# Convolution by pairs of tokens, VectorE in written order through the attention, and other places and times for output weights and norms, in one layer of a streaming encoder

## The chip, the cores and the metric

The kernel runs on one core of a Trainium2 chip. The metric is the device time of one execution in microseconds (us); lower is better. Before the change the median of three executions is 1045.45 us (1045.14 to 1045.65).

The engines are called as the profile calls them: PE multiplies matrices, DVE (VectorE), ACT (ScalarE) and POOL (GpSimd) work on whole tiles of 128 rows, SP only issues transfers (DMAs). Each has a queue of its own and works through it in order; semaphores tie the queues together. A DMA can add to its destination while it writes; this kernel issues those from POOL's queue.

## The reference, cut to what matters

One layer: an RMS norm, one input projection, and from its columns two branches.

```python
glu, q, k, v = project(rmsnorm(xp, norm_mix[l]), w_in[l])      # glu = a * sigmoid(b), 512 channels
glu_ext = concat([zeros((bsz, 30, 512)), glu], axis=1)         # or the last 30 rows of a running stream
a_out = silu(layernorm(depthwise_causal_conv(glu_ext, dw_w, dw_b)))   # 31 taps, each channel by itself
attn = prompt_attention(q, k, v, ...)                          # 16 chunks of 64 tokens, 8 heads, 16 meta tokens
xp = xp + concat([a_out, attn]) @ w_out[l]
```

Then follow a gated feed-forward (2816 wide, with a short convolution of its own) and a last norm. A second, small stream of 32 tokens with cached keys and values goes through the same layer. All values are float32. The kernel keeps tokens on the free axis: 16 meta tokens, 1024 prompt tokens and 32 of the running stream, 1072 columns, with channels on the 128 rows.

## The kernel before, in words

**Precision.** PE multiplies in a rounded form of float32, so each operand is split into a high and a low part, and each product is three matmuls: high by high, low by high, high by low (`mm3`, L257 to L262). A high part is a copy on ACT. A low part (value minus high part) is either one subtraction on DVE, or a negated copy on ACT followed by a transfer on POOL's queue that adds the value (`wload`, `wsplit`, L224 to L251).

**Input projection, 0 to about 160 us.** Columns of tokens are cut into three blocks `TB`. Weight tiles `c` = 0 to 13 are worked in a fixed order (`ORDER`): gate and value of convolution channels 0 and 1 first, then keys, values, channel 2, queries; the two weight tiles 6 and 7 of channel 3 are left for later. DVE takes the results out of PSUM (`in_evac`), and as soon as a channel `p` (128 rows of channels) has its gated value in a block, its convolution is put on a queue (`taps_of`, `conv_taps`): 31 taps, each one DVE instruction over the columns of a segment (`SEGS`), multiply by a weight and add (L405 the first, L408 the others). `taps(us)` issues taps worth about so many microseconds from up to two segments in turn. Twenty taps of one segment of channel 0 are done by ACT and adding transfers instead (`chain_taps`), and `chain_end` (L437) adds their two sums on DVE.

**Attention, about 164 to 248 us.** A loop of 20 rounds (L1012 on) carries 18 jobs: the meta tokens, 16 chunks, the running stream. In round `i` job `i` gets its scores on PE (L807), its bias and row minimum on DVE (`soft_a`, L762) and its exponentials on ACT (L769); job `i-1` gets its normalisation (`soft_b`, L774 and L777, or L779 where ACT does it: `SCA[i]` of four tiles), its transposes on PE (L826, L828) and their copies on ACT (L833); job `i-2` gets its output on PE (L842, L846) and the copy into `CA` on ACT (`keep`, L850). Between them PE does `FILL[i]` steps of the two left weight tiles (`glu_stream`; a step is three matmuls), first all blocks of tile 6, then all of tile 7. When these are done, `after_glu` splits `CA` and the second output weight tile, and PE starts on the output projection of the attention branch for block 0 (`ah_stream`, `AH[i]` steps in the last seven rounds). `taps(TA[i])` issues convolution taps at each round's end.

PE and ACT run in the order in which the program writes their instructions (`MANUAL`). DVE's order is chosen at build time by a list scheduler, in which taps have low priority and fill gaps.

**Output projection, about 248 to 345 us.** Twenty groups (L1123 on) multiply the attention half by output weight tiles `m2` = 0 to 3 for token blocks 1, 2 and 0. Each group is four steps, and each step is a tick. Ticks drive the layer norms of the convolution branch (`ln`, one for each block: sums, mean, squares, root, scaling, silu, split), which may begin at tick 14, with 21 ticks between beginnings and once their taps are issued. ACT copies each group's result out of PSUM (`ah_add`, L988), an adding transfer adds the layer's input. Then `conv_half` multiplies the normed convolution by the convolution half of the output weights (`whl`), in the order `WOC`, adds on DVE (L1170) and prepares the feed-forward. Three of these weight tiles are split only after the twenty groups (L1146), and the split tiles of the normed convolution (`CVH`, `CVL`) get their place when all three norms have summed their squares, by giving up the tile `glu` (`open_cv`).

Weight tiles pass through two raw buffers (`fetch`) and two pairs of high and low buffers; a third pair of uses waits for the first.

**Feed-forward, 345 us to the end.** Dense matmuls; the change does not touch it.

Of the kernel before, what the change touches and what calls it, by code (L numbers as in the profile page):

```python
# [18 lines left out]
P = 128  # L19
# [70 lines left out]
AFE = (0, 3, 18, 19)  # L90
GXW = FW - 1 + NPR + FW - 1 + NS
GOW = GXW - (FW - 1)
GS = NPR + FW - 1
# [81 lines left out]
def body(nc, tc, cp, wp, xp, dp, io):  # L175
# [10 lines left out]
    def close(cm):  # L186
        cm.__exit__(None, None, None)
# [209 lines left out]

    tapq, spare = [], [0.0, 0]

    def conv_taps(p, a0, a1, b):  # L400
        e, a = glu[:, p, :], acc[:, p, a0:a1]

        def tap(k):
            if k == 0:
                nc.vector.tensor_scalar(out=a, in0=e[:, a0:a1], scalar1=pcol("cw", p * CW), scalar2=pcol("cb", p),  # L405
                                        op0=ALU.mult, op1=ALU.add)
            else:
                nc.vector.scalar_tensor_tensor(out=a, in0=e[:, a0 + k:a1 + k], scalar=pcol("cw", p * CW + k),  # L408
                                               in1=a, op0=ALU.mult, op1=ALU.add)
# [26 lines left out]

    def chain_end():  # L437
        for a, half in chain:
            nc.vector.tensor_tensor(out=a, in0=a, in1=half, op=ALU.add)
        chain.clear()  # L440

    def taps(us, behind=None):
# [125 lines left out]
    def lead(c, b):  # L568
        return H0 if c >= 10 and b == 0 else 0
# [138 lines left out]
    def take(dst=None, dve=False):  # L708
        return wsplit(raws.pop(0), dst, dve)
# [205 lines left out]
            Chunk.keep(self, n=NS)  # L915

    def glu_stream():
        w = nxt
        for i, c in enumerate(order[NPRE:]):
            for b in range(3):  # L920
                for k, ps in enumerate(in_mm(b, w, lead(c, b))):
                    if k == 2 and b == 0:
                        wn = take()
                    if k == 2 and b == 1:
                        fetch()
                    if k == KD - 1:
                        pend.append((c, b, ps))
                    yield
            w = wn
        woas.append(w)  # L930
# [5 lines left out]
    def ca_split(b, k0, k1, dma=False):  # L936
        t0, n = OB[b]
        for k in range(k0, k1):
            if dma:
                nc.scalar.copy(CAH[b][:, k, :], CA[:, k, t0:t0 + n])  # L940
                nc.scalar.activation(CAL[b][:, k, :], CA[:, k, t0:t0 + n], AF.Copy, scale=-1.0)
            else:
                split(CAH[b][:, k, :], CAL[b][:, k, :], CA[:, k, t0:t0 + n])
        if dma:
            nc.gpsimd.dma_start(CAL[b][:, k0:k1, :], CA[:, k0:k1, t0:t0 + n], accum_op=ALU.add)

    def after_glu():
        nonlocal X, cX, cS
        close(cH)
        cX, px = pool("x1", "right")  # L950
        X = [new(px, f"x{b}", KD, n) for b, (t0, n) in enumerate(OB)]
        cS, pcs = pool("cas", "right")
        for b, (t0, n) in enumerate(OB):
            CAH.append(new(pcs, f"cah{b}", 4, n, dt=F32R))
            CAL.append(new(pcs, f"cal{b}", 4, n, dt=F32R))
        for step in AG:
            for op in step:
                if op == "h":
                    raw = raws.pop(0)
                    hi, lo = (wp.tile([P, 1024], F32R, tag=t, name=t) for t in ("whi", "wlo"))  # L960
                    nc.scalar.copy(hi, raw)
                elif op == "l":
                    nc.scalar.activation(lo, raw, AF.Copy, scale=-1.0)
                    nc.gpsimd.dma_start(lo, raw, accum_op=ALU.add)
                    woas.append((hi, lo))
                    fetch()
                else:
                    while op[0] == "1" and kept[0] < 11:
                        yield
                    ca_split(int(op[0]), int(op[1]), int(op[1]) + 2, op in CSD)  # L970
                    halved[0] += op[0] == "0"
            yield

    def halves(w):
# [34 lines left out]
    left = (len(order) - NPRE) * 3 * KD - PF  # L1009
    for _ in range(PF):  # L1010
        next(stream)
    for i in range(len(jobs) + 2):  # L1012
        job = jobs[i] if i < len(jobs) else None
        if a:
            a.soft_b(SCA[i])
        if job:
            job.scores()
            job.soft_a()
            job.exps(0)
            job.exps(1)  # L1020
# [12 lines left out]
        taps(TA[i], (job or a or z).q[1][3])  # L1033
        if not left and not pend and not defer:
            for _ in stream:
                pass
            next(later, None)
            ticks = len(jobs) + 2 - i
            for _ in range(AH[-ticks] if ticks <= len(AH) else 0):
                next(ahs, None)  # L1040
            for q in adds:
                ah_add(*q)
            adds.clear()
        if i == CHE:
            with tc.issue_after(job.q[1][3]):
                chain_end()
        z, a = a, job
    for _ in later:
        pass
    for _ in ahs:  # L1050
        pass
    for q in adds:
# [2 lines left out]
    def ln(b):  # L1055
# [31 lines left out]
        while not CVH:  # L1087
            yield 1
        for p in range(NCV):
            with tc.high_priority(offset=-1000000) if b else nullcontext():  # L1090
# [1 line left out]
                    split(CVH[b][:, p, lo_:hi_], CVL[b][:, p, lo_:hi_], acc[:, p, o:o + hi_ - lo_])  # L1092

    ca_split(2, 0, 4)
    close(cD)
    close(cA)
    lns = [ln(b) for b in range(3)]
    ticks, begun, due = [0], [], []

    def tick():  # L1100
        ticks[0] += 1
        for b, g in enumerate(lns):
            if len(due) == b:
                if ticks[0] < LN0 or begun and ticks[0] < begun[-1] + LNS or any(t[0] <= b for t in tapq):
                    return
                begun.append(ticks[0])
# [4 lines left out]
    whl, wres, squared, CVH, CVL = {}, [], [], [], []  # L1111

    def open_cv():
        nonlocal cG
        close(cG)
        cG, pd = pool("d3", "left")
        for b, (t0, n) in enumerate(OB):
            CVH.append(new(pd, f"cvh{b}", 4, n, dt=F32R))
            CVL.append(new(pd, f"cvl{b}", 4, n, dt=F32R))
        for m in range(2):  # L1120
            wres.append((new(pd, f"wrh{m}", 1024, dt=F32R), new(pd, f"wrl{m}", 1024, dt=F32R)))

    groups = [(m2, i, b) for m2 in range(2) for b in (1, 2) for i in range(2)]  # L1123
    groups += [(2, i, b) for i in range(2) for b in range(3)] + [(3, i, b) for b in range(3) for i in range(2)]
    for g, (m2, i, b) in enumerate(groups):
        if m2 not in woav:
# [12 lines left out]
        if len(squared) == 3 and not CVH:  # L1139
            open_cv()  # L1140
    if not CVH:
        taps(1e9)
        while len(squared) < 3:
            tick()
        open_cv()
    for m2 in WOC[1:]:  # L1146
        whl[m2] = halves(take((None, None, *wres)[m2], WLD))
        fetch()

    close(cS)  # L1150
    cH, ph = pool("h3", "right")
# [43 lines left out]
    region.__exit__(None, None, None)  # L1195
    close(cG)
    close(cC)
    cT, pt_ = pool("t", "left")
# [846 lines left out]
```

## Time and profile before

| | before |
|---|---|
| median of three executions | 1045.45 us |
| the profiled execution's own time | 1044.83 us |
| its span, first to last instruction | 1043.1 us |
| busy: PE, DVE, ACT, POOL | 1025.4, 880.8, 535.1, 189.5 us |
| convolution taps on DVE (L408), in 190 instructions | 155.3 us |
| granted TensorE clock | 0.998 |

The profiled execution is 0.62 us below the median, and 1.73 us of it lie outside the span. In the tables of stretches, each row is a stretch in us from the span's start, its length, the busy time of each engine with the number of instructions, the granted clock as a share, the busy share of the DMA engines and GB/s. In lists of groups, a row gives line, engine, operation, output and input, shape and count, then busy time and mean ns of one, then idle time ahead of them and what ended it. In lists of waits, a row gives who waited for whom, the total, the number of times, and the longest. In listings by time, a row begins with start and duration, and the time in square brackets is idle time ahead of it; durations of neighbours overlap a little, so the step from one to the next is somewhat shorter than the duration. Only PE's idle time lengthens the run for certain, since PE is busy for 98% of the span; idle time elsewhere counts where PE ends up waiting for it.

### The profile page before, as it was taken

Reading aid. Unit: us, or ns where it says so; the run is one execution under the profiler, and the core shown is the slowest. Engines: PE = TensorE matmul, PEld = TensorE weight load, DVE = VectorE, ACT = ScalarE, POOL = GpSimd, SP = SyncE. Lnnn points to the kernel's source line nnn. Section 1 sums busy time; section 2 is a strip of 40 time slices with the busy share of each in tenths; the row PEclk is TensorE's granted clock in tenths of the full one; section 3 lists DMA queues with packets and bytes.
Section 4 is the critical chain, followed back from the end, with each engine's and each line's share of the span. In section 5 each row is a group of like instructions: output and inputs, shape, how many; then the busy total and the mean of one; then the engine's idle time right before and its main releaser. Section 6 shows DMA issues by size and latency. Waiting matters only on the chain.

```text
span 1043.1 us, 20158 instructions
## 1 busy us (share of the span) xinstructions
PE 1025.4 (98%) x7699; PEld 999.2 (96%) x7699; DVE 880.8 (84%) x1723; ACT 535.1 (51%) x1146; POOL 189.5 (18%) x243
## 2 busy tenths in 40 slices
PE   9999999989999999999999999999999999999997
PEld 8999998758999999999999999999999999999997
DVE  7999988899978988989988989889888966986636
ACT  8653335897676744443543544445436722532334
POOL 1123120002425321020211111111100041000043
PEclk9999999999999999999999999999999999999999
DMA  7378673123963226244445445435536785732204
GB/s 269 90 167 162 148 151 89 41 52 62 168 165 106 81 83 158 73 130 144 117 129 156 121 123 155 132 114 146 152 93 231 247 171 138 252 122 81 83 1 167
DMA packets 77528, 137.39 MB, mean 132 GB/s; under 512 B 11248, under 2 KB 46184, under 8 KB 77432
## 3 DMA queue, kind: packets, MB, share of 16 engines
q1 hardware_dynamic: 58632, 100.96, 29.1%
q0 software_dynamic: 18368, 34.74, 19.7%
q8 instruction: 60, 0.98, 0.4%
q10 hardware_dynamic: 432, 0.41, 0.1%
q14 instruction: 36, 0.29, 0.1%
HBM read 81.52 MB, written 27.51 MB: 105 GB/s over the span
## 4 chain that ended last, share of the span: by engine, by line
PE 86%; ACT 6%; DVE 5%; DMA 2%; issue 1%; DVEq 0%; ACTq 0%
PE mm L1335 49%; PE mm L260 10%; PE mm L261 10%; PE mm L262 10%; PE mm L1546 3%; ACT pb L769 1%; DVE acc L408 1%; ACT glu L833 1%; PE R L297 1%; ACT hi L346 1%; PE R L1546 1%; PE R L276 1%; DMA raw<-woc 1%; DMA xs<-xT 0%; ACT glu L769 0%
## 5 line engine op out<-in xcount | busy, mean ns | idle before, releaser
L408 DVE SCALAR_TENSOR_TENSOR acc<-glu,prm,acc 128x324 f32<-128x324 f32 (+4 forms) x190 | 155.3, 847 | 1.1
L1335 PE MATMUL mm<-bh,sl 128*128 128x264 f32 (+1 forms) x664 | 148.4, 285 | 0.3 <-DVE x L1482 0.3
L1335 PE MATMUL mm<-bh,wlo 128*128 128x264 f32 (+1 forms) x560 | 134.5, 284 | 0.0
L1335 PE MATMUL mm<-th,rawr 128*128 128x264 f32 x640 | 122.5, 284 | 0.0
L1335 PE MATMUL mm<-bl,sl 128*128 128x264 f32 (+1 forms) x424 | 120.6, 284 | 0.0
L1335 PEld LDWEIGHTS mm<-bh,sl 128*128 128x128 f32 x664 | 112.1, 188 | 0.6 <-DVE x L1482 0.5
L260 PE MATMUL mm<-hi,whi 128*128 128x352 f32 (+3 forms) x312 | 104.0, 333 | 0.6 <-ACT hi L346 0.6
L1482 DVE TENSOR_TENSOR x<-x,mm 128x264 f32<-128x264 f32 (+7 forms) x222 | 69.4, 343 | 41.3 <-PE mm L1335 41.1
L261 PE MATMUL mm<-lo,whi 128*128 128x352 f32 (+3 forms) x312 | 101.3, 325 | 0.2 <-DVE lo L347 0.2
L1335 PEld LDWEIGHTS mm<-th,rawr 128*128 128x128 f32 x640 | 101.4, 188 | 0.0
L262 PE MATMUL mm<-hi,wlo 128*128 128x352 f32 (+3 forms) x312 | 101.2, 324 | 0.0
L1335 PEld LDWEIGHTS mm<-bh,wlo 128*128 128x128 f32 x560 | 97.8, 188 | 0.0
L1335 PE MATMUL mm<-tl,rawr 128*128 128x264 f32 x320 | 90.9, 284 | 0.0
L1223 ACT CAST sl<-x 128x512 fp32r<-128x512 f32 (+2 forms) x66 | 40.0, 608 | 95.1 <-PE mm L1335 79.7
L1335 PE MATMUL mm<-th,sl 128*128 128x264 f32 x344 | 85.9, 284 | 0.0
L1335 PEld LDWEIGHTS mm<-bl,sl 128*128 128x128 f32 x424 | 79.8, 188 | 0.0
L1335 PE MATMUL mm<-th,wlo 128*128 128x264 f32 x272 | 77.3, 284 | 0.0
L1335 PE MATMUL mm<-tl,sl 128*128 128x264 f32 x272 | 77.2, 284 | 0.0
L1335 PE MATMUL mm<-bh,whi 128*128 128x264 f32 (+1 forms) x312 | 71.8, 284 | 0.0
L1335 PEld LDWEIGHTS mm<-th,sl 128*128 128x128 f32 x344 | 61.0, 188 | 0.2 <-ACT gx L1480 0.2
L260 PEld LDWEIGHTS mm<-hi,whi 128*128 128x128 f32 x312 | 58.7, 188 | 1.8 <-ACT hi L346 0.8
L1335 PEld LDWEIGHTS mm<-tl,rawr 128*128 128x128 f32 x320 | 60.3, 188 | 0.0
(442 smaller groups left out, 3070.4 us busy)
## 6 DMA issues: line engine op xcount, KB each, us to landing
x<-wup SPq DMA_DIRECT2D x48, 256.0 KB, 2.8
yq<-x SPq DMA_DIRECT2D x46, 264.0 KB, 3.0
x<-wup SPq DMA_DIRECT2D x20, 512.0 KB, 3.4
wlo<-raw POOLq DMA_DIRECT2D x16, 512.0 KB, 4.6
ca<-ca POOLq DMA_DIRECT2D x18, 383.0 KB, 5.2
raw<-win SPq DMA_DIRECT2D x12, 512.0 KB, 4.7
raw<-wdn SPq DMA_DIRECT2D x12, 512.0 KB, 6.6
rb<-yq SPq DMA_DIRECT2D x10, 528.0 KB, 4.7
```

The costliest lines, as they stand in the source:

```text
L260: nc.tensor.matmul(ps, whi(k), xhi(k), start=first and i == 0, stop=False)
L261: nc.tensor.matmul(ps, whi(k), xlo(k), start=False, stop=False)
L262: nc.tensor.matmul(ps, wlo(k), xhi(k), start=False, stop=last and i == n - 1)
L276: nc.tensor.matmul(ss[:, i:i + 1], z[:, at:at + P], ones[:, 0:1], start=j == 0, stop=j == len(parts) - 1)
L297: nc.tensor.matmul(R[:, at:at + P], left[i], diag[i], start=True, stop=True)
L346: hid[b, k] = nc.scalar.activation(HI[b][:, k, :], X[b][:, k, :], AF.Copy, scale=pcol("g1", k)).ins
L408: nc.vector.scalar_tensor_tensor(out=a, in0=e[:, a0 + k:a1 + k], scalar=pcol("cw", p * CW + k), in1=a, op0=ALU.mult, op1=ALU.add)
L769: nc.scalar.activation(qs_[i], qs_[i], AF.Exp, bias=m[0][:, i:i + 1], scale=-1.0, accum_out=m[1][:, i:i + 1])
L1223: nc.scalar.copy(hi, raw)
L1335: nc.tensor.matmul(ps, w[:, j, :], x[:, j, :], start=first and j + i == 0, stop=j == 3 and i == 2, skip_group_check=True)
L1482: summed[0] = nc.vector.tensor_tensor(out=z, in0=z, in1=ps[:, lo_:hi_], op=ALU.add).ins
L1546: nc.tensor.matmul(ps, z[:, j, :], x[:, j, :], start=q in FIRST and j + i == 0, stop=j == 1 and i == 2, skip_group_check=True)
```

## The change

- **Pairs.** For channels 1 and 2 and the longer part of channel 3, the 31 taps over all columns become 48 instructions over half as many columns, reading and writing every second column. With a weight array of differences, even and odd outputs share the products of odd weights with sums of neighbouring inputs.
- **Written order.** In the attention loop DVE runs in the program's order too. Low parts, results out of PSUM and taps move ahead of the outputs and transposes in each round; results out of PSUM are taken one round later. `TA` is smaller.
- **Attention's side work.** Six rounds leave all normalisation to DVE. Low parts of `CA` and of three weight tiles go to DVE; their negated copies and adding transfers go. `glu_stream` takes block by block both tiles instead of tile by tile. `chain_end` becomes two adding transfers, two rounds earlier.
- **Output weights and norms.** The third output weight tile gets buffers of its own. The first eight groups go block by block. The convolution's weights are split after groups 13, 15 and 17 and at the end, two of them with adding transfers. Norms begin at ticks 15, 39, 59. Block 0 of the normed convolution has its place from the start; the others come over `glu`.

```diff
-TA = [2.01, 2.74, 5.63, 6.64, 4.22, 3.28, 2.42, 2.68, 2.08, 1.57, 2.08, 2.08, 3.18, 1.41, 2.1, 0.85, 4.71, 3.21, 5.98, 2.57]
+TA = [0.0, 0.0, 2.0, 1.0, 1.9, 1.5, 2.0, 1.5, 1.2, 1.2, 0.4, 1.0, 0.5, 1.0, 0.5, 0.9, 0.9, 1.2, 3.0, 3.0]
-WOC = (0, 2, 1, 3)
-WLD = True
+WOC = (0, 2, 3, 1)
+WLD = (False, False, True, True)
-SCA = [1, 2, 2, 2, 1, 1, 2, 2, 2, 2, 2, 1, 2, 2, 0, 1, 1, 2, 2, 2]
-LN0 = 14
-LNS = 21
+SCA = [1, 2, 2, 2, 1, 1, 2, 2, 2, 2, 2, 1, 0, 0, 0, 0, 0, 0, 2, 2]
+LNT = (15, 39, 59)
-CHE = 5
+CHE = 3
-SEGS = (((0,), (1, 2)), ((0, 1, 2),), ((0, 1, 2),), ((0,), (1,), (2,)))
-CSD = ['12', '00']
+SEGS = (((0,), (1, 2)), ((0, 1, 2),), ((0, 1, 2),), ((0,), (1, 2)))
+PAIRS = ((1, 0), (2, 0), (3, 1))
+NP2 = CW // 2
-AG = (('00', '02'), ('h',), ('l',), ('10',), ('12',))
-AT = (1, 8)
-AT2 = 13
-AFE = (0, 3, 18, 19)
+AG = (('00',), ('02',), ('h',), ('l', '10'), ('12',))
+AT = {1: True, 8: False}
+AT2 = {13: 0, 15: 2, 17: 3}
+AFE = (0, 2, 9, 14, 16)
...
+    def pair_taps(p, a0, a1, b):
+        n = (a1 - a0) // 2
+        sums = pair_place(p, n + NP2 - 1)
+        y = [acc[:, p, a0 + i:a1:2] for i in range(2)]
+
+        def e(k, m=n):
+            return glu[:, p, a0 + k:a0 + k + 2 * m - 1:2]
+
+        def one(out, x, w, into):
+            nc.vector.scalar_tensor_tensor(out=out, in0=x, scalar=w, in1=into, op0=ALU.mult, op1=ALU.add)
+
+        def tap(k):
+            i, j = k
+            if i == 0:
...
+                nc.vector.tensor_tensor(out=sums, in0=e(1, m), in1=e(2, m), op=ALU.add)
+            elif i == 1:
+                w, x = pcol("cw", p * CW + 2 * j + 1), sums[:, j:j + n]
+                if j == 0:
+                    nc.vector.tensor_scalar(out=y[1], in0=x, scalar1=w, scalar2=pcol("cb", p), op0=ALU.mult,
+                                            op1=ALU.add)
+                else:
+                    one(y[1], x, w, y[1])
+            elif i == 2:
+                w = pcol("cw", p * CW) if j == 0 else pdif[:, p - 1, 0, j - 1:j]
+                one(y[0], e(2 * j), w, y[0] if j else y[1])
+            else:
+                w = pdif[:, p - 1, 1, j:j + 1] if j < NP2 else pcol("cw", p * CW + CW - 1)
+                one(y[1], e(2 * j + 1), w, y[1])
+
+        ks = [(0, 0), *((1, j) for j in range(NP2)), *((i, j) for j in range(NP2 + 1) for i in (2, 3))]
+        tapq.append([b, n, tap, ks, p])
...
     def chain_end():
         for a, half in chain:
-            nc.vector.tensor_tensor(out=a, in0=a, in1=half, op=ALU.add)
+            nc.gpsimd.dma_start(a, half, accum_op=ALU.add)
...
+    def low(lo, x, hi):
+        lows.append(lambda: nc.vector.tensor_tensor(out=lo, in0=x, in1=hi.bitcast(F32), op=ALU.subtract))
...
+            hi, lo, x = CAH[b][:, k, :], CAL[b][:, k, :], CA[:, k, t0:t0 + n]
+            nc.scalar.copy(hi, x)
+            low(lo, x, hi)
...
+    region.__exit__(None, None, None)
+    region = tc.manual_schedule(engines=MANEND)
+    region.__enter__()
     for i in range(len(jobs) + 2):
...
+        low_parts()
+        flush()
+        taps(TA[i])
         if z:
             z.outs()
         if a:
...
-        flush()
-        taps(TA[i], (job or a or z).q[1][3])
-        if not left and not pend and not defer:
+        if not left:
             for _ in stream:
                 pass
+            flush()
+            flush()
             next(later, None)
...
-    groups = [(m2, i, b) for m2 in range(2) for b in (1, 2) for i in range(2)]
+    groups = [(m2, i, b) for b in (1, 2) for m2 in range(2) for i in range(2)]
...
         if g in AT:
-            woas.append(take())
-        if g == AT2:
-            whl[0] = halves(take(dve=WLD))
+            woas.append(take(wthird if AT[g] else None))
+        if g in AT2:
+            conv_weights(AT2[g])
```

More of the change, by code (lines that the diff above doesn't have):

```diff
@@ L398, in body, with pair_place @@
     tapq, spare = [], [0.0, 0]
+    pdif = cp.tile([P, NCV - 1, 2, NP2], F32, tag="pdif", name="pdif")
+    co = PRM["cw"][0] + CW
+    wv = prm[:, co:co + (NCV - 1) * CW].rearrange("p (a b) -> p a b", b=CW)
+    nc.gpsimd.tensor_tensor(out=pdif[:, :, 0], in0=wv[:, :, 2::2], in1=wv[:, :, 1::2], op=ALU.subtract)
+    nc.gpsimd.tensor_tensor(out=pdif[:, :, 1], in0=wv[:, :, 0:CW - 1:2], in1=wv[:, :, 1::2], op=ALU.subtract)
+    def pair_place(p, n):
+        return (None, acc[:, 3, ACCW - n:], acc[:, 3, 0:n], glu[:, 2, 0:n])[p]
+    def pair_taps(p, a0, a1, b):
[9 more added lines that the diff above has]
+            if i == 0:
+                assert not any(q[4] == p - 1 and (p == 3 or len(q[3]) > 2 * (NP2 + 1)) for q in tapq if q[2] is not tap)
+                m = n + NP2 - 1
+                nc.vector.tensor_tensor(out=sums, in0=e(1, m), in1=e(2, m), op=ALU.add)
[14 more added lines that the diff above has]
+        tapq.append([b, n, tap, ks, p])
     def conv_taps(p, a0, a1, b):
+        if (p, b) in PAIRS:
+            pair_taps(p, a0, a1, b)
+            return
         e, a = glu[:, p, :], acc[:, p, a0:a1]
@@ L917, in glu_stream @@
     def glu_stream():
[L918 to L925, printed above, removed]
+        cs = order[NPRE:]
+        ws = {cs[0]: nxt}
+        for b in range(3):
+            for c in cs:
+                for k, ps in enumerate(in_mm(b, ws[c], lead(c, b))):
+                    if k == 2:
+                        if c == cs[0]:
+                            if b == 0:
+                                ws[cs[1]] = take(dve=True)
+                        elif b < 2:
+                            fetch()
+                        else:
+                            wn = take(dve=True)
                     if k == KD - 1:
@@ L934, in body, with low_parts, ca_split @@
     CAH, CAL, woas = [], [], []
-    def ca_split(b, k0, k1, dma=False):
+    lows = []
+    def low(lo, x, hi):
+        lows.append(lambda: nc.vector.tensor_tensor(out=lo, in0=x, in1=hi.bitcast(F32), op=ALU.subtract))
+    def low_parts():
+        while lows:
+            lows.pop(0)()
+    def ca_split(b, k0, k1):
         t0, n = OB[b]
         for k in range(k0, k1):
[L939 to L945, printed above, removed]
+            hi, lo, x = CAH[b][:, k, :], CAL[b][:, k, :], CA[:, k, t0:t0 + n]
+            nc.scalar.copy(hi, x)
+            low(lo, x, hi)
     def after_glu():
@@ L961, in after_glu @@
                     nc.scalar.copy(hi, raw)
+                    low(lo, raw, hi)
                 elif op == "l":
-                    nc.scalar.activation(lo, raw, AF.Copy, scale=-1.0)
-                    nc.gpsimd.dma_start(lo, raw, accum_op=ALU.add)
                     woas.append((hi, lo))
@@ L1044, in body @@
         if i == CHE:
-            with tc.issue_after(job.q[1][3]):
-                chain_end()
+            chain_end()
         z, a = a, job
@@ L1086, in ln @@
         yield LNW[6]
-        while not CVH:
+        while b >= len(CVH):
             yield 1
@@ L1094, in body @@
     ca_split(2, 0, 4)
+    low_parts()
     close(cD)
@@ L1109, in tick, with conv_weights @@
                 due[b] = ticks[0] + next(g, 1000)
-    whl, wres, squared, CVH, CVL = {}, [], [], [], []
-    def open_cv():
[L1114 to L1121, printed above, removed]
-    groups = [(m2, i, b) for m2 in range(2) for b in (1, 2) for i in range(2)]
+                if len(squared) == 3 and len(CVH) == 1:
+                    open_cv()
+    whl, squared = {}, []
+    cV, pd = pool("d3", "left")
+    CVH, CVL = ([new(pd, f"{z}0", 4, OB[0][1], dt=F32R)] for z in ("cvh", "cvl"))
+    cvl2 = new(pd, "cvl2", 4, OB[2][1], dt=F32R)
+    wres = [(new(pd, f"wrh{m}", 1024, dt=F32R), new(pd, f"wrl{m}", 1024, dt=F32R)) for m in range(2)]
+    wthird = new(pd, "w3h", 1024, dt=F32R), new(pd, "w3l", 1024, dt=F32R)
+    def open_cv():
+        n1, n2 = 4 * OB[1][1], 4 * OB[2][1]
+        z = pg.tile([P, 2 * n1 + n2], F32R, tag="glu", name="cv")
+        for to, a, n in ((CVH, 0, n1), (CVL, n1, n1), (CVH, 2 * n1, n2)):
+            to.append(z[:, a:a + n].rearrange("p (a b) -> p a b", a=4))
+        CVL.append(cvl2)
+    def conv_weights(m2):
+        whl[m2] = halves(take((None, None, *wres)[m2], WLD[WOC.index(m2)]))
+    groups = [(m2, i, b) for b in (1, 2) for m2 in range(2) for i in range(2)]
     groups += [(2, i, b) for i in range(2) for b in range(3)] + [(3, i, b) for b in range(3) for i in range(2)]
@@ L1138, in body @@
         taps(TH)
[L1139 to L1148, printed above, removed]
+    taps(1e9)
+    while len(due) < 1 or due[0] < 1000:
+        tick()
+    conv_weights(WOC[3])
     close(cS)
```

17 lines of the change are left out of this document (10 added, 7 removed).

## The prediction

> **What bounds the kernel now.** I read the page first, then busy time by stretches, then PE's waits inside the stretches that the change touches.
>
> ```profile
> span 1043.1 us, 20158 instructions
> PE 1025.4 (98%) x7699; PEld 999.2 (96%) x7699; DVE 880.8 (84%) x1723; ACT 535.1 (51%) x1146; POOL 189.5 (18%) x243
> ```
>
> PE is idle for 1043.1 - 1025.4 = 17.7 us of the whole run. The change adds and removes no matmul, so it can gain at most what of these 17.7 us lies in its stages. The stretches show where (columns: PE, weight loads, DVE, ACT, POOL):
>
> ```profile
> 140.00:164.00 24.00, 24.00 (x153) 23.78 (x151) 22.85 (x25) 8.77 (x11) 6.08 (x8) 1.00 0.75 154
> 164.00:200.00 36.00, 34.13 (x249) 27.27 (x250) 29.40 (x111) 28.43 (x97) 0.85 (x1) 1.00 0.25 60
> 200.00:220.00 20.00, 18.61 (x138) 13.49 (x134) 19.89 (x76) 18.25 (x62) 1.21 (x1) 1.00 0.02 3
> 220.00:248.00 28.00, 24.35 (x185) 17.95 (x186) 27.81 (x97) 26.11 (x83) 3.30 (x3) 1.00 0.39 72
> ...
> 260.00:270.00 10.00, 10.00 (x65) 9.87 (x63) 9.51 (x22) 4.92 (x13) 4.96 (x5) 1.00 0.98 183
> ...
> 300.00:310.00 10.00, 9.18 (x60) 8.68 (x60) 7.56 (x14) 8.36 (x18) 1.79 (x3) 1.00 0.57 203
> ```
>
> Before 164 us PE has no gap left. The attention, 164 to 248 us, leaves 1.87 + 1.39 + 3.65 = 6.9 us idle, and there DVE is busy 77.1 of 84 us and ACT 72.8. The output projection loses 0.82 us. Together 7.7 us can be won: the ceiling. PE's waits by cause, first for 165 to 250 us and then for 250 to 360 us:
>
> ```profile
> PE o L842 <- ACT ca L850: 3.5, 9, 0.8
> PE pt L826 <- ACT pb L779: 1.3, 2, 0.9
> PE pt L826 <- DVE glu L777: 1.0, 1, 1.0
> PE o L907 <- ACT ca L850: 0.8, 1, 0.8
> ```
>
> ```profile
> PE mm L260 <- DVE x L1170: 0.8, 2, 0.6
> ```
>
> These are 6.6 of the 6.9 us. 5.6 us of them end with ACT being late (the outputs wait for the copies of the round before, the transposes for a normalisation on ACT) and 1.0 us with DVE. So ACT bounds this stage, with DVE just behind: ACT's exponentials wait in turn for DVE's minima.
>
> **Pairs.** The taps as DVE did them (widths 1090, 384 and 324), and their whole:
>
> ```profile
> 161.41 2.74 DVE L408 SCALAR_TENSOR_TENSOR acc<-glu,prm,acc 128x1090 f32<-128x1090 f32 x2
> ...
> 210.21 2.08 DVE L408 SCALAR_TENSOR_TENSOR acc<-glu,prm,acc 128x324 f32<-128x324 f32 x4
> ...
> 223.38 1.61 DVE L408 SCALAR_TENSOR_TENSOR acc<-glu,prm,acc 128x384 f32<-128x384 f32 x3
> ```
>
> ```profile
> L408 DVE SCALAR_TENSOR_TENSOR acc<-glu,prm,acc 128x324 f32<-128x324 f32 x30 | 16.5, 550 | 0.2
> L408 DVE SCALAR_TENSOR_TENSOR acc<-glu,prm,acc 128x384 f32<-128x384 f32 x26 | 16.0, 616 | 0.0
> L408 DVE SCALAR_TENSOR_TENSOR acc<-glu,prm,acc 128x1090 f32<-128x1090 f32 x6 | 8.1, 1349 | 0.0
> L408 DVE SCALAR_TENSOR_TENSOR acc<-glu,prm,acc 128x382 f32<-128x382 f32 x7 | 4.3, 620 | 0.0
> L439 DVE TENSOR_TENSOR acc<-acc,ca 128x766 f32<-128x766 f32 x2 | 1.9, 954 | 0.0
> L777 DVE TENSOR_SCALAR pb<-pb,sm 128x209 f32<-128x209 f32 x25 | 7.3, 326 | 0.1
> L762 DVE CUSTOM_DVE_ANT_0 pb<-S,bt 128x209 f32<-128x209 f32 x41 | 13.6, 371 | 0.2 <-PE S L807 0.2
> L774 DVE RECIPROCAL sm<-sm 128x4 f32<-128x4 f32 x16 | 2.8, 175 | 2.9 <-ACT glu L769 2.5 <-ACT pb L769 0.2
> ```
>
> Neighbours overlap by about 0.1 us, so one tap costs about 1.3 us at 1090 columns, 0.53 at 384 and 0.5 at 324: some 1.07 ns a column and 0.12 us fixed. A pair tap of 545 columns comes to 0.70 us, one of 383 to 0.53. Channels 1 and 2 go from 31 x 1.3 = 40 us each to 48 x 0.70 = 34, the longer part of channel 3 from 31 x (0.53 + 0.53) = 33 to 48 x 0.53 = 25. That is 20 us less of DVE. No row here reads every second float, so this price is bounded: below by the rate just used, above by half that rate (two columns' time for one), 1.3 us for 545 and 0.93 for 383. I take the lower end, since all wide taps lie on one line in width and nothing in them depends on being contiguous that the trace shows. [...]
>
> None of these 20 us lies on PE's path before 164 us, since PE never waits there. What they do is clear DVE's backlog: the six taps of 1090 columns above, 8.1 us, belong to channel 2 and run inside the attention. With 12 us less to do before, they should be finished at its start. With them goes the one wait of PE for DVE, whose cause shows in the order of time: the normalisation stood behind a long tap.
>
> ```profile
> 171.01 1.34 DVE L408 SCALAR_TENSOR_TENSOR acc<-glu,prm,acc 128x1090 f32<-128x1090 f32 x1
> 172.27 0.25 DVE L777 TENSOR_SCALAR glu<-glu,sm 128x81 f32<-128x81 f32 x1
> ```
>
> Gain 1.0 us.
>
> **DVE's load in the attention.** Now it carries 16.5 + 16.0 + 8.1 + 4.3 = 44.9 us of taps. The new `TA` sums to 24.7. Added are eight normalisations (8 x 0.33 = 2.6 us) and low parts: two of 324 and two of 384 columns, and two of 1024 inside the loop (a third falls just before it); the one of 1024 that the trace has took 1.22 us (row below), so 2 x 0.45 + 2 x 0.5 + 2 x 1.2 = 4.3. `chain_end` takes 1.9 away. DVE goes from 77.1 to about 77.1 - 44.9 + 24.7 + 2.6 + 4.3 - 1.9 = 62 of 84 us. It is no longer near full, which is what written order needs: DVE can no longer fill its waits.
>
> ```profile
> L247 DVE TENSOR_TENSOR wlo<-raw,whi x2: 1219/1222/1226, 281.4 to 296.5; 128x1024 fp32r<-128x1024 f32 x2
> ```
>
> **ACT's load in the attention.** Rows of one round and of its neighbours:
>
> ```profile
> 218.76 0.83 ACT L779 ACTIVATE pb<-pb,sm 128x209 f32<-128x209 f32 x2
> ...
> 220.34 1.05 ACT L833 COPY glu<-pt 128x512 f32<-128x512 f32 x2
> 221.28 0.38 ACT L850 COPY ca<-o 128x256 f32<-128x256 f32 x1
> ...
> 223.17 0.47 ACT L769 ACTIVATE pb<-pb,sm 128x209 f32<-128x209 f32 x1
> ...
> 223.62 0.47 ACT L769 ACTIVATE glu<-glu,sm 128x209 f32<-128x209 f32 x1
> ...
> 225.72 1.07 ACT L963 ACTIVATE wlo<-raw 128x1024 fp32r<-128x1024 f32 x1
> ...
> 234.22 0.55 ACT L941 ACTIVATE cal<-ca 128x384 fp32r<-128x384 f32 x1
> ```
>
> Four exponentials step by 0.45, so a round holds 1.8 + 0.95 + 0.3 = 3.05 us, and each normalisation 0.37 more. In rounds 12 to 17 eight normalisations leave ACT (3.0 us), with one negated copy of 1024 columns (1.0) and, in rounds 11 to 15, four of `CA` (1.6): 5.6 us less just where most of the ACT waits lie. Two more negated copies (2.0 us) go elsewhere. I don't take all of it. Waits like this one lie in rounds 4 to 8, which keep their two normalisations:
>
> ```profile
> 189.93 0.65 PE L842 MATMUL o<-glu,va 128*64 128x256 f32 x4 [0.29 <-ACT ca L850]
> ```
>
> Four of them are an estimated 1.0 us. And in rounds 12 to 15 ACT still has 3.05 us and some 0.9 of high parts, 4.0 us. PE's 77.1 busy us over 20 rounds are 3.9 each, but these rounds hold at most two steps where others hold three to six. I leave 1.0 us there. ACT's waits fall from 5.6 to 2.0.
>
> **The added order.** In each round the reciprocal stands first in DVE's queue and waits for the last exponential of the job before; behind it wait four normalisations, the minima, low parts, results out of PSUM and taps. For PE to notice, the normalisations must come later than the scores and outputs that PE has ahead of the transposes, about 2 us. Only in round 11 is a wait added that I can name: the last results of tile 7 are taken in the same round, so DVE stands until PE's last step. I charge 0.4 us, between 0 and 1. Moving the adding transfers from DVE to POOL (`chain_end`) and dropping the others costs nothing on PE's path: PE reads none of them before the norms, and POOL is busy 0.85 + 1.21 + 3.30 us of 84.
>
> **Output projection.** Taps left over there now, by stretch:
>
> ```profile
> 248.00:260.00 12.00, 7.12 (x13) 1.00 0.49 73
> 260.00:270.00 10.00, 6.63 (x11) 1.00 0.98 183
> 270.00:280.00 10.00, 3.77 (x7) 1.00 0.69 142
> ```
>
> 17.5 us. After: the pairs' 25 and block 0's 31 x 0.5 = 15.5 of channel 3, less the 24.7 of `TA`: 16 us. They all precede the second norm, which may begin at tick 39, four ticks later than the earliest before (14 + 21). A step is three matmuls, 0.46 us by the row above (65 in 10 us), so that is 2 us, while DVE is as full as it is now (9.51 of 10). I charge 0.5 us, between 0 and 2. The 0.8 us wait for L1170 came after three weight tiles that were split together behind the groups; these now come earlier, and block 0's split before tick 80. I take it as won. New is that two convolution tiles use an adding transfer, which holds their raw buffer:
>
> ```profile
> wlo<-raw POOLq DMA_DIRECT2D x6, 512.0 KB, 4.6
> raw<-woc SPq DMA_DIRECT2D x4, 512.0 KB, 6.5
> ```
>
> After group 13 the buffer is taken for 2 us of ACT, 4.6 and then up to 6.5 for the next load: 13 us, while group 17 ends 16 steps, 7.4 us, and the norms' matmuls later. ACT then stands for some 4 us, with the copies of groups 18 and 19 behind it. PE has three PSUM banks, 12 steps or 5.5 us of work. Cost 0, bound 2. The third tile's own buffers end a wait of ACT that cost PE nothing.
>
> **Sum.** Gained 1.0 (long tap) + 3.6 (ACT) + 0.8 (L1170) = 5.4, lost 0.4 + 0.5 = 0.9: 4.5 us. The profiled execution's own time is 1044.83 us, 1.73 of it outside the span and untouched; less 4.5 it is 1040.3. The median of the runs shown lies 0.62 above it, so 1040.9.
>
> **The rivals.**
>
> *Little is won.* ACT stays the bound, because the work per round that remains (3.05 us and high parts) still exceeds PE's, or the second norm and the raw buffer take 2 us each. Against it: 5.6 us leave ACT where it is late. For it: ACT is busy 26.11 of 28 us in the worst stretch. Gain 1 us: 1044.5.
>
> *DVE in written order becomes the bound.* From exponentials to exponentials the chain is serial: 1.8 us on ACT, then on DVE a reciprocal (0.2), four normalisations (4 x 0.33, less overlaps, 1.0) and the first minimum (0.4), 3.4 us with no hand-over. Taps or results that are still running when the exponentials end come on top. If they add over 1 us in a round, the round passes what PE can fill. At 0.5 us in each of 16 rounds that is 8 us lost, with the 0.5 of the second norm, against 5.4 gained: 1045.45 + 3.1 = 1048.5. It decides by whether DVE's reciprocal waits for ACT (then it does not) or PE's transposes wait for L777. [...] Against it stand 22 us of free time.
>
> *Strided taps at half rate.* Then pairs cost 48 x 1.3 = 62 us a channel, 22 more than now, in a stage where DVE has 1 us free in 24. 40 us of backlog would stand in written order ahead of the first softmax, and PE would wait for most of it, 30 us: 1075.5. Against it: every width measured lies on one line, so what a tap costs looks like columns and nothing else.
>
> **How the numbers follow.** Forecast 0.66, little won 0.15, written order 0.13, half rate 0.04, something unnamed 0.02. 0.2% is 2.1 us, about what a measurement of this kernel can tell. The forecast's own range is from the ceiling, 1045.45 - 7.7 = 1037.7, to 1043. Faster by more than 2.1 us (below 1043.4): the forecast and a little of the second, 0.70. Within: most of the second, a fifth of the third, 0.14. Slower: 0.16. The range reaches from the ceiling over the second rival and the milder half of the third, 1037.7 to 1047.
>
> **What would show it.** In the changed profile PE's idle time from 164 us to the end of the attention falls from 6.9 to about 2.5 us, with no `pt <- L777` entry of note; DVE is busy about three quarters there and waits for ACT ahead of the reciprocal; taps of 545 columns take about 0.75 us as listed; L408 and its pair lines sum to about 135 us; no tap of channel 2 starts after the first scores. The output projection shows no `L1170` wait and under 1 us at the second norm's first matmul. I am wrong if PE waits for L777 in most rounds, if a 545-column tap takes over 1 us, or if ACT's waits are as long as before.

## The result, and the profile after

| | before | after |
|---|---|---|
| median | 1045.45 us | 1056.38 us (1055.26 to 1057.08, five executions) |
| profiled execution, its span | 1044.83, 1043.1 us | 1057.08, 1055.3 us |
| PE busy, idle in the span | 1025.4, 17.7 us | 1029.0, 26.3 us |

The changed kernel is slower: ratio 1.0102, interval 1.0087 to 1.0117. The forecast was 1040.9 us, range 1037.7 to 1047.0.

The page of the changed kernel: span, busy time by engine, and the clock row over 40 slices of 26 us.

```profile
span 1055.3 us, 20172 instructions
...
PE 1029.0 (98%) x7699; PEld 1003.2 (95%) x7699; DVE 867.6 (82%) x1754; ACT 531.8 (50%) x1133; POOL 184.6 (17%) x244
...
PEclk9999999999989999999999999999999999999999
```

The number of matmuls is the same, yet PE is busy 3.6 us longer and idle 8.6 us longer, 12.2 us of span together. Longer busy time at equal work points to the clock: one slice of 26.4 us, the twelfth, shows an 8. The stretches, in the columns of before:

```profile
164.00:200.00 36.00, 35.21 (x258) 28.25 (x258) 28.15 (x114) 26.60 (x93) 0.85 (x1) 1.00 0.17 38
200.00:220.00 20.00, 17.43 (x134) 12.85 (x131) 15.39 (x64) 16.89 (x55) 0.00 (x0) 1.00 0.09 28
220.00:248.00 28.00, 25.54 (x196) 19.72 (x195) 27.40 (x98) 24.01 (x77) 1.70 (x2) 1.00 0.16 32
260.00:270.00 10.00, 9.59 (x62) 9.30 (x61) 10.00 (x25) 4.40 (x9) 3.55 (x3) 1.00 0.81 147
270.00:280.00 10.00, 8.97 (x58) 8.42 (x56) 7.62 (x16) 7.62 (x17) 2.11 (x2) 1.00 0.75 149
290.00:300.00 10.00, 1.26 (x8) 0.96 (x7) 3.36 (x6) 2.63 (x6) 1.20 (x1) 0.82 1.01 225
300.00:310.00 10.00, 9.35 (x45) 9.35 (x46) 2.87 (x8) 4.19 (x10) 2.24 (x3) 0.67 0.22 60
```

Idle time in the attention went from 6.9 us to 0.79 + 2.57 + 2.46 = 5.8. It fell by 1.1 us before 200 and by 1.2 after 220, and rose by 1.2 between. The output projection, which lost 0.8 us before, now loses 0.4 + 1.0 + 8.7 + 0.65 = 10.8 in the rows shown; and where the clock stands at 0.82 and 0.67, PE does its work more slowly on top. PE's waits name the place:

```profile
PE S L276 <- DVE glu L1135: 9.8, 2, 9.4
PE o L888 <- ACT ca L896: 3.9, 6, 1.2
PE pt L872 <- DVE glu L823: 1.4, 1, 1.4
...
PE S L1127 <- DVE glu L1124: 1.0, 1, 1.0
```

The wait of 9.4 us is PE's matmul that sums the third norm's squares. Followed backwards, the chain that ended last runs through it so (start, length, what):

```profile
283.51 7.26 DMA wlo<-raw
...
290.82 6.99 DMA raw<-woc
...
297.83 1.05 ACT wrh L245
...
298.91 1.23 DVE wrl L247
300.13 0.48 DVE glu L1135
...
300.65 1.44 PE S L276 x6
```

Two transfers of half a megabyte follow each other because they share a raw buffer: the adding transfer of the convolution's first tile reads it until 290.8, and only then can the load of the third tile start. ACT's high part of that tile stands in written order and waits. DVE's low part waits for it, and behind that, in DVE's queue, stands the last sum of the third norm. On DVE this order is not the program's: outside the attention the scheduler chooses it. The program writes that sum at tick 66 and the split of the tile after tick 72, and the scheduler put the low part first. PE's queue is in written order, so it cannot go on with the groups that are ready. ACT's and DVE's rows show the same from their side (idle time ahead in brackets):

```profile
297.83 1.04 ACT L245 CAST wrh<-raw 128x1024 fp32r<-128x1024 f32 x1 [7.37 <-DMA raw<-woc]
```

```profile
298.91 1.23 DVE L247 TENSOR_TENSOR wrl<-raw,wrh 128x1024 fp32r<-128x1024 f32 x1 [6.64 <-ACT wrh L245]
```

### The profile page after: what moved, and what is told of

The parts are those of the page before. It is cut to its first block, busy times and chain, and to the rows that moved or that the text cites. A ratio compares the mean times of both kernels' runs of the same rounds, so it can differ in the third digit from the quotient of the medians.

```text
span 1055.3 us, 20172 instructions
## 1 busy us (share of the span) xinstructions
PE 1029.0 (98%) x7699; PEld 1003.2 (95%) x7699; DVE 867.6 (82%) x1754; ACT 531.8 (50%) x1133; POOL 184.6 (17%) x244
## 4 chain that ended last, share of the span: by engine, by line
PE 87%; DVE 6%; ACT 4%; DMA 3%; issue 1%; POOL 0%; DVEq 0%; ACTq 0%; POOLq 0%; SPq 0%
PE mm L1401 48%; PE mm L260 10%; PE mm L261 9%; PE mm L262 9%; PE mm L1612 3%; DVE acc L418 1%; DMA wlo<-raw 1%; DMA raw<-woc 1%; PE R L297 1%; ACT hi L346 1%; PE R L1612 1%; ACT glu L879 1%; DMA xs<-xT 1%; PE o L888 1%; ACT pb L815 1%
## 5 line engine op out<-in xcount | busy, mean ns | idle before, releaser
L260 PE MATMUL mm<-hi,whi 128*128 128x384 f32 (+3 forms) x312 | 104.1, 334 | 0.3 <-ACT hi L346 0.3
L261 PE MATMUL mm<-lo,whi 128*128 128x384 f32 (+3 forms) x312 | 101.3, 325 | 0.2 <-DVE lo L347 0.2
L262 PE MATMUL mm<-hi,wlo 128*128 128x384 f32 (+3 forms) x312 | 101.2, 324 | 0.0
L418 DVE SCALAR_TENSOR_TENSOR acc<-glu,pdif,acc 128x545 f32<-128x545 f32 (+1 forms) x90 | 60.1, 724 | 0.0
```

Of the source, the lines that this page charges most:

```text
L260: nc.tensor.matmul(ps, whi(k), xhi(k), start=first and i == 0, stop=False)
L261: nc.tensor.matmul(ps, whi(k), xlo(k), start=False, stop=False)
L262: nc.tensor.matmul(ps, wlo(k), xhi(k), start=False, stop=last and i == n - 1)
L418: nc.vector.scalar_tensor_tensor(out=out, in0=x, scalar=w, in1=into, op0=ALU.mult, op1=ALU.add)
```

## The experiments

The theory after the trace: the raw buffer held by the adding transfer costs the 9.4 us, and the half clock after it some 3 more; the rest of the missed gain lies in the attention and in the norms' ticks. The rivals: the stall would come in any case because the norms begin when they do; or the pairs do not pay; or VectorE's written order costs by itself. Each comparison with before is made with executions of before on the same chip at the same time (medians 1045.45, 1045.61 and 1045.48 us in the three sets).

### The adding transfers taken away

```diff
-WLD = (False, False, True, True)
+WLD = (True, True, True, True)
```

All low parts of the convolution's tiles are made on DVE.

> The changed kernel, with the low parts of all four convolution weight tiles on DVE instead of two of them by adding transfers. Theory (raw buffer): the adding transfer of tile 0 held its raw buffer until 290.8 us, so the load of tile 3 landed at 297.8, ACT and then DVE stood for it, and PE's third norm with them: 9.4 us idle and about 2.9 us at half clock. With the buffer given back by DVE some 7 us earlier, the 9.4 us wait falls below 1 us, the clock stays at 1.0 and the time comes to 1044 to 1046. Rival (place: the split of tile 3 after group 17 is too early whoever makes the low part): the wait stays over 4 us and the time over 1049. Rival (attention): the loss is in written order, and the time stays over 1052.

Measured: 1049.61 us, 1.0030 (1.0019 to 1.0042), 6.8 us less than the changed kernel. PE's waits:

```profile
PE S L276 <- DVE glu L1135: 3.1, 2, 2.7
```

Without adding transfers the 9.4 us are 2.7, so most of the wait hangs on them. The theory's 1044 to 1046 us was missed all the same: a low part of 1.22 us still stands ahead of the norm's sum in DVE's queue, and after the wait the clock is still low for a while (0.50 from 296 to 298 us, 0.83 over 290 to 300).

### The third tile split two groups later

```diff
-AT2 = {13: 0, 15: 2, 17: 3}
+AT2 = {13: 0, 15: 2, 19: 3}
```

Nothing else differs; both adding transfers stay.

> The changed kernel, with the split of the third convolution weight tile after group 19 instead of 17; adding transfers and buffers as in the change. Theory (raw buffer, and the order behind it): the load still lands at about 298, but nothing of the third norm stands behind it on ACT and DVE any more; PE's wait at the norm goes, a wait of up to 2 us comes in the convolution half, time 1044 to 1047. Rival (the load alone decides, whatever stands behind it): PE still waits 6 us or more near 300 us, time over 1051.

Measured: 1047.83 us, 1.0020 (1.0011 to 1.0029), 8.6 us less than the changed kernel. The buffer is held as long as before, but nothing that PE needs stands behind it. So a transfer that holds the buffer cost PE only because its end was waited for ahead of the norm's sum, by ACT in written order and by DVE in the scheduler's. Written order on DVE in this stage too, which would have kept the sum ahead, was not tried. A wait of 1.53 us at the same matmul is left.

### PE kept busy through the stall

```diff
+        if b == 2:
+            for _ in range(40):
+                nc.tensor.matmul(flat(pts[0])[:, 0:P], ones, ones, start=True, stop=True)
```

Forty matmuls on constants, whose result nothing reads, fill PE's time ahead of the third norm's sum (the trace counts each as two: its stretches hold some 80 matmuls more than those of the two runs above); ACT and DVE wait for the transfers as in the changed kernel.

> The changed kernel, with 40 extra small matmuls on constants (nobody reads them) on PE ahead of the third norm's sums, so that PE works through most of its 9.4 us wait. The wait's end is set by the load and does not move. Theory (idle PE loses clock, and the loss is a price of its own): the granted clock stays near 1.0 in 296 to 306 us, and the time falls by 2 to 3 us to about 1053.8. Rival (the low clock is no cost or has another cause): time stays within 0.8 us of 1056.4 or rises by what the extra matmuls take, and the clock falls as before.

Measured: 1053.34 us, 1.0071 (1.0056 to 1.0086). The clock in the two stretches (PE alone):

```profile
290.00:300.00 10.00, 10.00 (x90) 1.00 0.99 232
300.00:310.00 10.00, 10.00 (x71) 1.00 0.53 133
```

Where it was 0.82 and 0.67, it is 1.00 now, and the median is 3.0 us lower. The stall is not quite the same: PE starts the norm's matmuls 8.8 us after its last step, not 9.4. The clock alone is read from there to the convolution half, over the same matmuls (first the changed kernel, then this one):

```profile
300.65 1.44 PE L276 MATMUL S<-ones,glu 128*128 128x1 f32 x6 [9.40 <-DVE glu L1135]
...
306.50 0.36 PE L260 MATMUL mm<-cvh,whi 128*128 128x324 f32 x1
```

```profile
299.83 0.73 PE L276 MATMUL S<-ones,glu 128*128 128x1 f32 x6
...
302.90 0.31 PE L260 MATMUL mm<-cvh,whi 128*128 128x324 f32 x1
```

That is 5.85 us against 3.07: the half clock costs 2.8 us.

### The pairs alone, in the kernel before

```diff
+PAIRS = ((1, 0), (2, 0))
```

The kernel before with pair taps for channels 1 and 2, its order and all else as it was.

> The kernel before, with only the pairs of channels 1 and 2 added. Theory (pairs work at full rate but lie off PE's path): taps of 545 columns take about 0.78 us as listed, DVE does 11 to 12 us less, PE's 1.0 us wait behind a long tap goes, and the time falls by 0 to 1.5 us, to 1044 to 1045.5. Rival (pairs are what the change lives by): 3 us or more faster, under 1042.5. Rival (pairs cost through contention or strided access): over 1047.

Measured: 1046.76 us, 1.0012 (1.0003 to 1.0022). The stretches of the attention (columns: PE, weight loads, DVE, ACT, POOL):

```profile
164.00:200.00 36.00, 35.32 (x260) 28.10 (x258) 24.45 (x108) 28.73 (x98) 1.43 (x2) 1.00 0.24 60
200.00:220.00 20.00, 18.62 (x140) 13.79 (x138) 19.89 (x74) 18.26 (x62) 1.21 (x1) 1.00 0.04 6
220.00:248.00 28.00, 24.37 (x186) 17.62 (x182) 27.81 (x97) 25.73 (x80) 3.39 (x4) 1.00 0.39 73
```

The gain of 1.2 us before 200 (34.13 to 35.32) is the pairs'; after 200 nothing changes (18.61 to 18.62, 24.35 to 24.37), with DVE as full as before. The median does not show the 1.2 us: by the trace PE begins the feed-forward 0.7 us earlier (343.59, not 344.29) and starts its last matmul 1.2 us later (1037.01, not 1035.82), in code that is the same. In part this is a wait that the kernel before does not have, for the low part of a weight tile in the feed-forward:

```profile
PE mm L264 <- DVE wlo L1272: 0.7, 1, 0.7
```

Why it comes, and the rest of the 1.9 us, is not settled.

### Norms at other ticks

```diff
-LNT = (15, 39, 59)
+LNT = (17, 43, 63)
```

On top of the later split of the third tile.

> The changed kernel with the third convolution tile split after group 19 and the three norms begun at ticks 17, 43 and 63 instead of 15, 39 and 59. Theory: what is left against the kernel before, 1047.83 with the late split alone, is the norms' own: TensorE stands 0.41, 1.01 and 1.53 us before their sums, and the half clock after the last of these costs 1.6 us more: 4.5 us in all, so about 1043.3, with no wait on the sums of the norms left and the granted clock at 1.00 from 280 to 300 us. Rival: the norms are late for what follows them, and the waits turn up at the convolution's outputs: 1046 to 1048 as before.

Measured: 1047.58 us, 1.0021 (1.0010 to 1.0032): no better than the later split alone. The rival had the time, and the place in part: 0.8 us of wait are back at the convolution's outputs. The second norm's 1.0 us is gone, 1.1 us are left before the sums, but another wait has come:

```profile
PE S L297 <- ACT diag L291: 3.2, 1, 3.2
...
PE S L276 <- DVE glu L1135: 1.1, 2, 0.6
...
PE mm L260 <- DVE x L1235: 0.8, 1, 0.8
```

The third norm's last products wait for ACT's diagonals, and these stand behind the high part of the last convolution tile, whose raw buffer is again held by an adding transfer. The same mechanism, one tile further on. How long it lasts varies: the profiled execution took 1049.08 us, 1.5 over the median, and in the next three runs the same wait is 1.0 to 1.2 us. This kernel is the base of those three and of the last run.

### The streamed tile's low part left to the next round

```diff
-                            wn = take(dve=True)
+                            raw = raws.pop(0)
+                            wn = tuple(wp.tile([P, 1024], F32R, tag=t, name=t) for t in ("whi", "wlo"))
+                            nc.scalar.copy(wn[0], raw)
+                            low(wn[1], raw, wn[0])
```

In the attention of the changed kernel DVE meets a low part for which ACT's high part is not ready, and PE then waits for the normalisation queued behind it (DVE's row, then PE's):

```profile
209.15 1.23 DVE L247 TENSOR_TENSOR wlo<-raw,whi 128x1024 fp32r<-128x1024 f32 x1 [1.59 <-ACT whi L245]
```

```profile
210.88 0.33 PE L872 MATMUL pt<-ident,glu 128*128 128x128 f32 x1 [1.37 <-DVE glu L823]
```

> As c_norms_later, and the low part of the streamed tile in the attention is left to the next round's low parts instead of being written where its tile is taken. Theory: in VectorE's written order that low part waits for ScalarE's high part (1.59 us at 209) and holds up what stands behind it, from which TensorE's 1.37 and 1.20 us near 211 and 215 come: both go, 2.6 us less than c_norms_later. Rival: the low part is then late for the products that read it and TensorE waits for it there instead: no gain, or up to 1 us more.

Measured: 1045.96 us, 1.0006 (0.9996 to 1.0015), 1.6 us less than its base. The theory had 2.6. The wait of 1.37 us is gone, and the stretch from 200 to 220 has 18.80 us of PE instead of 17.43; of the other wait that the theory named, 1.20 us for ACT's copy of an output, 1.00 is left:

```profile
200.00:220.00 20.00, 18.80 (x144) 13.90 (x140) 16.99 (x70) 18.16 (x61) 0.00 (x0) 1.00 0.09 29
```

### VectorE's written order undone

```diff
-    region = tc.manual_schedule(engines=MANEND)
+    region = tc.manual_schedule(engines=MANUAL)
```

> As c_norms_later, with VectorE taken out of the written order in the attention's rounds (TensorE and ScalarE stay in it). Theory: the written order as such costs only the two waits at 211 and 215 us: without it they go, and up to 2.6 us are won. Rival, my forecast's own: the order only cost 0.4 us net, because without it VectorE's sums come in a worse order elsewhere: within 0.5 us of c_norms_later, either way.

Measured: 1048.23 us, 1.0032 (1.0021 to 1.0044); the intervals overlap its base's. The stretches show why no net effect is seen:

```profile
200.00:220.00 20.00, 18.86 (x145) 13.94 (x141) 13.92 (x63) 18.89 (x63) 0.00 (x0) 1.00 0.10 29
220.00:248.00 28.00, 24.07 (x175) 18.16 (x176) 27.96 (x97) 22.01 (x70) 1.22 (x1) 1.00 0.12 27
```

Against the base (17.43 and 25.52) the middle wins 1.43 us, the end loses 1.45. So the written order is worth some 1.5 us at the attention's end, and loses them in the middle, where the run with the low part deferred won 1.37. The theory named only the loss, the rival only the sum.

### ScalarE's relief undone

```diff
-SCA = [1, 2, 2, 2, 1, 1, 2, 2, 2, 2, 2, 1, 0, 0, 0, 0, 0, 0, 2, 2]
+SCA = [1, 2, 2, 2, 1, 1, 2, 2, 2, 2, 2, 1, 2, 2, 0, 1, 1, 2, 2, 2]
```

> As c_norms_later, with the softmax normalisation of rounds 12 to 17 put back on the engines of the kernel before. Theory: the relief of ScalarE in those rounds is worth what TensorE's waits there fell by, from about 5.1 to 2.2 us: 2.9 us slower than c_norms_later. Rival: VectorE pays for it in the same rounds, and nothing changes: within 0.5 us.

Measured: 1047.31 us, 1.0017 (1.0008 to 1.0027), no slower than its base:

```profile
220.00:248.00 28.00, 25.60 (x193) 19.64 (x192) 26.28 (x90) 25.22 (x81) 2.02 (x2) 1.00 0.16 32
```

PE's 25.60 stands against 25.52 with the relief. ACT has 1.3 us more to do in this stretch, DVE 1.1 less, and PE does not notice. The theory falls.

### All mends together

All low parts of the convolution's tiles on DVE, the third tile split after group 19, norms at ticks 17, 43 and 62, the streamed low part deferred.

> The changed kernel with four mends: all low parts of the convolution's tiles on VectorE, its third tile split after group 19, the norms begun at ticks 17, 43 and 62, the streamed tile's low part in the attention deferred to the next round. Theory: with the low parts on VectorE no adding transfer holds the staging buffer, the last weight tile lands sooner, and ScalarE's diagonals of the third norm no longer stand behind its high part: the 1.06 us before the third norm's last products go, and with them the range of the runs narrows: 1044 to 1045, at or a little under the kernel before. Rival: VectorE's own low parts push the third norm's sums back, and TensorE waits there instead: 1046 to 1047.

Measured: 1043.61 us, 0.9980 (0.9971 to 0.9989). No wait for the diagonals is left. The same with the norms at 17, 42 and 60:

> As d1_best_of_all with the norms begun at ticks 17, 42 and 60. Theory: about a tick is left to either side: the sums of the third norm are waited for again for some 0.5 to 1 us, and its diagonals come free of the last tile's high part: within 1 us of d1_best_of_all. Rival: a wait on the sums of over 1.5 us halves the clock again: 2 us or more slower.

Measured: 1044.41 us, 0.9990 (0.9981 to 0.9999), with a wait of 0.9 us before the third norm's sums; as the theory said. And the same as the first of these with the softmax normalisation of rounds 12 to 17 on the engines of before:

> As d1_best_of_all with the softmax normalisation of rounds 12 to 17 put back on the engines of the kernel before. Theory, after the last runs: the relief is worth nothing, since what ScalarE gives up VectorE has to do in the same rounds: within 0.5 us. Rival: with the low part deferred VectorE has room, and the relief shows: 1 to 3 us slower than d1_best_of_all.

Measured: 1041.84 us, 0.9967 (0.9954 to 0.9979), 1.8 us less than with the relief: neither theory nor rival had the sign. But the attention does not show it; PE's busy time there, first with the relief, then without (PE alone):

```profile
164.00:248.00 84.00, 79.79 (x591) 1.00 0.16 34
```

```profile
164.00:248.00 84.00, 79.82 (x592) 1.00 0.16 34
```

The spans of the two lie 1.1 us apart. Of these, 0.5 is a wait for a low part in the feed-forward (`PE mm L262 <- DVE wlo L1293`) that only the kernel with the relief has. What the relief has to do with the 1.8 us is not shown. This kernel is faster than both kernels of the case, by 3.6 and 14.5 us. Its page and its waits:

```profile
span 1040.1 us, 20167 instructions
...
PE 1025.5 (99%) x7699; PEld 999.9 (96%) x7699; DVE 866.6 (83%) x1748; ACT 532.2 (51%) x1139; POOL 185.7 (18%) x242
```

```profile
PE o L888 <- ACT ca L896: 3.4, 7, 1.0
...
PE S L276 <- DVE glu L1138: 0.5, 1, 0.5
```

PE is idle for 1040.1 - 1025.5 = 14.6 us, 3.1 less than before, with its busy time as before; the stall and the half clock are gone (clock 1.00 from 260 to 310 us).

### Single taps in the new order

```diff
-PAIRS = ((1, 0), (2, 0), (3, 1))
+PAIRS = ()
```

On the base with the later norms; `TA` and the ticks stay as they are, and channel 3's longer part is single too.

> As c_norms_later with the taps taken one at a time instead of in pairs. Theory: the pairs take some 14 us off VectorE, of which the attention and the stretch after it use only what lets the taps end before the second norm: with single taps the second norm starts later, TensorE waits there, and the long tap's wait of 1.0 us is back: 1.5 to 4 us slower than c_norms_later. Rival: the taps are hidden anyway: within 0.5 us.

Measured: 1059.28 us, 1.0136 (1.0120 to 1.0151), 11.7 us more than its base, far over the 1.5 to 4 of the theory.

```profile
PE S L1127 <- DVE glu L1124: 4.4, 1, 4.4
...
PE pt L872 <- DVE pb L823: 2.0, 1, 2.0
```

With single taps DVE is late for the second norm by 4.4 us and for the attention's first rounds by 2.0, and after each of them the clock is lower for a time (0.68 from 280 to 290 us, 0.91 from 180 to 200). Channel 1's and 2's pairs won nothing in the old order; the new one, with its `TA` and ticks as set, depends on having pairs. Other settings for single taps were not tried.

## Why the prediction was wrong

**The step that failed** is the raw buffer: "After group 13 the buffer is taken for 2 us of ACT, 4.6 and then up to 6.5 for the next load: 13 us", then "ACT then stands for some 4 us", "PE has three PSUM banks, 12 steps or 5.5 us of work. Cost 0, bound 2." The mechanism was there and its length nearly: from 281.2 us, when ACT's high part began, to 297.8 it took 16.6, since the transfers took 7.26 and 6.99, not 4.6 and 6.5, and ACT stood 7.4 us. What failed is the cover. The three banks were to let PE work on while ACT's copies are late, but PE stopped at something else: a matmul of the third norm that stands between its steps, in written order. It needs a sum on DVE, which stood behind a low part on DVE, where the scheduler had put it, and that waited for ACT. Who queues behind the waiting instruction was asked for ACT and not for DVE. Price: 9.4 us of idle time and, as the filled stall shows, 2.8 us of half clock; 12.2 where 0 stood. Splitting the tile later took back 8.6 of it.

**ScalarE's relief, "3.6 (ACT)"**, was wrong as well. PE waits 3.9 + 0.3 us for the copies of the outputs after, 3.5 + 0.8 before, where 2.0 in all were forecast for waits that end with ACT; the 1.3 us at the transposes that ended with ACT are now 1.4 that end with DVE. Undone alone, the relief costs nothing; undone in the mended kernel, PE's busy time in the attention stays at 79.8 of 84 us. "ACT bounds this stage" was read from the last releaser of PE's waits. But exponentials wait for minima on DVE, outputs for transposes after DVE's normalisations: the chain goes through both engines, and moving some 3 us from one to the other did not shorten it.

**The written order, "0.4, between 0 and 1"**: about 0 net, but of two effects of 1.4 to 1.5 us, by the run with the order undone. The low part at 209.15 waits 1.59 us for ACT, and PE's 1.37 us follow. The low parts were counted as load (1.2 us each) and not as waits.

**The second norm, "0.5, between 0 and 2"**: 1.0 us, gone when it begins four ticks later. Mechanism and bounds held. A further 0.4 us at the first norm's sum was not foreseen.

**The pairs** were priced rightly. The pair taps of the changed kernel, by shape:

```profile
L418 DVE SCALAR_TENSOR_TENSOR acc<-glu,pdif,acc 128x545 f32<-128x545 f32 x60 | 43.3, 781 | 0.0
...
L418 DVE SCALAR_TENSOR_TENSOR acc<-glu,pdif,acc 128x383 f32<-128x383 f32 x30 | 16.8, 611 | 0.0
```

781 ns as listed, where about 750 were named and over 1000 as the sign of half rate. A pair tap of 383 columns takes 611 ns, where a single tap of 382 neighbouring columns took 620 in the attention before: at this width every second float costs no more, and that rival falls. The long tap's wait (1.0 us) and L1170's (0.8) went as forecast. DVE's load in the attention was not: 28.15 + 15.39 + 27.40 = 70.9 us busy, where 62 were worked out. The sum took 44.9 us of listed tap times off a busy total that counts overlaps once; 69 taps that overlap by about 0.1 us are an estimated 7 us too much. Low parts also rose by 5.6 us as listed, where 4.3 were added; the rest is not assigned.

**Put together**: forecast gain 5.4, less 0.9. What came, in the profiled runs: 1.1 in the attention and 0.8 at L1170 won; 1.4 at the norms, 9.4 of stall and 2.8 of clock lost: 11.7 us, against 12.2 of span. The rest, 0.5 us, is not assigned. Two signs that were named failed: PE's idle time in the attention fell to 5.8 us and not to 2.5, and DVE is busy for 84% of it and not for three quarters.

The rival on the slow side (DVE's written order, 1048.5) looked at the right engine: what came was a late operand on DVE that held up all behind it, 9.4 us for PE. But it had the wrong stage, and a price for many small waits, not one long one.

## What to carry to other kernels

When an instruction is given a new wait, follow what is queued behind it on its own engine, then on each engine that waits for those, until every chain ends. Follow it in the order that was built: here a scheduler had put the waiting low part ahead of a sum that the program writes first. A cover such as free PSUM banks counts only if PE's next instruction in its order needs nothing of that chain; here one that did need it stood for 9.4 us. The raw buffer was held until its last reader ended, and a transfer that reads it is such a reader: 7.3 us here, to 290.8, when the next load began, instead of 1.2 on DVE. And the engine that ends a wait need not be what bounds a stage in which two engines take turns: moving work between them won nothing here.

## What the runs showed of the hardware

A pause of PE cost twice here. After the 9.4 us the matmuls came every 0.29 us instead of 0.15 to 0.17 until 306.5 us, 2.8 us in all. The clock had halved at about 296.4, 5.1 us into the pause, and came back at about 306.6; with the pause filled it stayed at 1.00. A far shorter pause was followed by the half clock as well: with the third tile split later PE stood 1.53 us to 292.40, and then (2-us stretches, PE alone, clock in the fifth place)

```profile
290.00:292.00 2.00, 0.87 (x6) 1.00 1.16 217
...
294.00:296.00 2.00, 2.00 (x9) 0.50 1.04 289
```

the clock was halved from 294.0 to 297.4, some 3.4 us, though PE was busy throughout. Yet with the later norms PE stood 3.21 us, and the clock stayed:

```profile
300.00:302.00 2.00, 0.81 (x6) 1.00 0.94 292
302.00:304.00 2.00, 0.00 (x0) 1.00 0.10 37
304.00:306.00 2.00, 1.98 (x14) 1.00 0.55 66
```

So in these runs the length of a pause does not decide alone: 1.53 us were followed by a clock of 0.50, 3.21 us by one of 1.00. No run shows what else counts; whether it is the six one-column matmuls of the norm right behind the pause of 1.53 us was not tried.
